# A four-layer trunk with ConvFFN: a shift read as a scalar from PSUM, and two adaLN sections moved from TensorE to VectorE

## The chip, the core and the metric

The kernel runs on one core of a Trainium2 chip. The metric is device time in microseconds from one execution of the whole program; lower is better. The core has five engines with queues of their own: TensorE (PE; matmul), VectorE (DVE), ScalarE (ACT), GpSimd (POOL) and SyncE (SP), which issues the loads. They meet through semaphores.

## The reference

One step of a trunk of four layers over 128 context tokens and 256 latent tokens with 1024 features. Each layer has a token mixer (gated MLP, pooling, attention, gated MLP) and a ConvFFN, and both are preceded by an RMSNorm with a shift and a scale and followed by a gate. These six vectors of a layer ("adaLN sections" of 1024 values, for two conditions) come from one large product. What matters here:

```python
def ada_params(cond, w, b):
    m = jax.nn.silu(cond) @ w + b
    return jnp.split(m[:, None, :], 6, axis=-1)

def conv_ffn(h, w_in, conv_w, conv_b, w_out):
    a, u = jnp.split(h @ w_in, 2, axis=-1)
    ap = jnp.pad(a, ((0, 0), (1, 1), (0, 0)))
    a = ap[:, :-2] * conv_w[0] + ap[:, 1:-1] * conv_w[1] + ap[:, 2:] * conv_w[2] + conv_b
    return (jax.nn.gelu(a) * u) @ w_out

def run_trunk(x, cond, is_context, cache_k, cache_v, weights):
    ...
        sh1, sc1, gt1, sh2, sc2, gt2 = ada_params(cond, w_ada[i], b_ada[i])
        h = rms_norm(x, g_mix[i]) * (1 + sc1) + sh1
        ...
        x = x + gt1 * y
        h = rms_norm(x, g_ffn[i]) * (1 + sc2) + sh2
        x = x + gt2 * conv_ffn(h, w_ffn_in[i], ffn_conv_w[i], ffn_conv_b[i], w_ffn_out[i])
```

Context tokens use one condition and latent tokens another; the inner width of the ConvFFN is 2816.

## The kernel before

Features lie on partitions, the 384 tokens along the free axis (`T` = 384). Every weight product runs in three passes of float32 parts (`mm3`, L631): high by high, low by high, high by low. The weights come as chunks of 128 x 1024, 582 in all, in the one order that `chunk_plan` (L90) writes down; SP loads them in that order (`load`, L313) into five buffers, so a chunk's place in the plan sets when it arrives. ScalarE rounds a weight chunk to its high part (`whi`, L338) and VectorE takes the remainder (`wlo`, L345), both in `w_split`, up to three chunks ahead of TensorE (`w_get`).

Among the weights stand the chunks of the adaLN sections. The table `ADA` (L39) says for each phase of a layer which sections, or which of a section's eight chunks, come along, and on which engine. "ad" goes to VectorE (`ada_dve`, L374): two instructions over 128 x 1024 with an accumulated sum (L380), a *pair* below. "ap" goes to TensorE (`ada_pe`, L389): four column-tiled products into one PSUM tile (L398), and after a section's last chunk a copy by ScalarE (L402), two transposes (L421) and an addition by VectorE. `weave` (L75) spreads the chunks evenly over the phase's weights, but for those at the edges (`EDGES`; in phase "fi" none after the last six weight chunks). After each `w_split` VectorE works off the pairs that have arrived (L348); `w_get` places the products of "ap" ahead of the next weight chunk's.

The phases used below are, for layer l: "fi" (first product of the ConvFFN, 22 feature tiles f of a and of u), "fo" (its second product), "nm" and "qkv" (norm, and the query/key/value product of the attention in layer 2; blocks b = 0, 2, 1 in this order, 2 holds the keys and values).

In `ffn` (L641) the norm's factor follows after the product: the operand holds x times its gain, next to two columns `T:TE` with the shift, so the PSUM tiles pa and pu hold the product and, in their last two columns, that of the shift for the two groups of tokens. The factor comes late: `stats` (sums of squares by TensorE, `ms` L524, the root), a diagonal R (L530) on VectorE, a product that spreads it over the partitions (`spread`, L536), and a copy to `rbs`. A pool of six PSUM banks holds pa and pu. Their epilogue, by feature: `epi_a` (a = pa x rbs, L657; the shifts' columns copied to `be`, L659 and L660; u = pu x rbs, L662), `epi_b` (on ScalarE a + shift into `ab` and the middle tap, on VectorE the two other taps `ct`, L676), `epi_c` (gelu on ScalarE, then gg = (u + shift of u) x gelu on VectorE, one instruction for each group, L685), and the split of gg into `gh` and `gl` (L567, L568). The epilogue of f runs while TensorE works on f + 1; that of f = 0 and 1 both while it works on f = 2, since the first four tiles (two features) are computed together.

Of the kernel before, what the change touches and what calls it, by code (L numbers as in the profile page):

```python
# [20 lines left out]
T = 384  # L21
# [15 lines left out]
# adaLN sections (layer, which of the six) computed along with the weights of a phase: by VectorE ("ad", features on  # L37
# partitions, dot products along the free axis) or by TensorE ("ap", column-tiled products)
# [18 lines left out]
# chunks of a phase that none of VectorE's sections follow, at its start and at its end  # L57
EDGES = {(0, "gv"): (2, 1), (0, "go"): (5, 0), (3, "gv"): (5, 2), "fi": (0, 6), (3, "go"): (5, 2)}

# the same for those of TensorE, at the end  # L60
# [4 lines left out]
# ---------------------------------------------------------------- packing  # L65


def out_chunks(fam, j, nk):
    """Two feature tiles at a time, but the last two one after the other."""
    n = (nk + 3) // 4  # L70
    return [(fam, j, m, kk) for m in range(3) for kk in range(n)] + [(fam, j, m, kk) for m in (3, 4)
                                                                    for kk in range((nk + 7) // 8)]


def weave(ws, es, lead, rest):  # L75
    """Spread es evenly over ws, but for the first `lead` and the last `rest`."""
    out, n, i = [], 0, 0
    total = sum(w[0] not in ("ad", "ap") for w in ws)
    for w in ws:
        out.append(w)  # L80
        if w[0] in ("ad", "ap"):
            continue
        i += 1
        m = min(len(es), max(0, len(es) * (i - lead) // max(1, total - lead - rest)))
        out += es[n:m]
        n = m
    return out


def chunk_plan():  # L90
    """Chunks of 128 x 1024 in the order in which the program loads them: (family, index)."""
# [126 lines left out]
def shape_consts():  # L218
    """Constants that depend on shapes alone: rope tables, window mask, a selection matrix."""
# [20 lines left out]
def pool_mix():  # L240
    """mix[t', g, t]: weight of token t' in the centred mean at t, less one where t' = t."""
# [17 lines left out]
def pool_sums():  # L259
    """Column sums of mix for each group of tokens (what a shift common to all its tokens is weighed with)."""  # L260
# [7 lines left out]
# ---------------------------------------------------------------- program  # L268


class Prog:
# [36 lines left out]
    # ---- stream of chunks  # L308
# [4 lines left out]
    def load(self, most=BUFS):  # L313
        """Start the loads for which there is room."""
# [14 lines left out]
    def w_split(self, upto, mid=None):  # L329
        """Round the coming chunks (ScalarE), run mid, take the remainders (VectorE)."""  # L330
# [38 lines left out]
    # ---- adaLN parameters  # L369
# [37 lines left out]
    def ada_spare(self, n):  # L407
        """At most n of VectorE's chunks, of those already loaded."""
# [19 lines left out]
    def ada_fill(self, n, fin=True):  # L428
        """At most n products of those already loaded; without fin, none that would have to close a section before."""
# [17 lines left out]
    # ---- norm  # L447
    def residual(self, d, ps, l, ty, after):
        """x_d += gate * ps, and what follows from x_d."""
# [9 lines left out]
    def square(self, d, acc):  # L459
        """Add the squares of x_d to acc; the last ones are only returned."""  # L460
# [18 lines left out]
    def rsqrt_steps(self, m, shape, y):  # L479
        """1/sqrt(m) by VectorE alone: an estimate from the exponent, refined to float32; one instruction at a time."""  # L480
# [22 lines left out]
    def rsqrt(self, m, shape):  # L503
        """1/sqrt(m), refined to float32."""
# [10 lines left out]
    def stats(self, *parts):  # L515
        """1/rms of each token (tokens on partitions) from tiles that add up to the squares."""
# [10 lines left out]
    def diag(self, r):  # L527
        """A diagonal of r for each token tile."""
# [10 lines left out]
    def gains(self, l, which):  # L539
        """g * (1 + sc) for both groups."""  # L540
# [8 lines left out]
    def put(self, ks, A, rb, hi, lo, l):  # L549
        """hi and lo of x * A * rb + B for some tiles."""  # L550
# [19 lines left out]
    def prep(self, l, which, extra=None):  # L570
        """What a norm's product needs of x_d, right after x_d is there: its squares, and x * g * (1 + sc) split in
        two, next to the shift's columns; the norm's factor follows after the product."""
# [24 lines left out]
    def norm(self, l, pr, bank):  # L597
        """Returns put(n), which makes h = rms_norm(x) * g * (1 + sc) + sh for the next n tiles."""
# [19 lines left out]
    def prep_squares(self, l):  # L618
        """The squares alone, for a norm before its product."""
# [10 lines left out]
    # ---- matrix products  # L630
    def mm3(self, outs, whl, rhl, first, last, nw=128):  # L631
        """Three passes for a set of (psum, weight column) with one k: hi*hi, lo*hi, hi*lo."""
# [7 lines left out]
    # ---- feed forward  # L640
    def ffn(self, l, pr, follow, stat_k):  # L641
        nc = self.nc
        hh, hl = self.hh[:, :, 0:TE], self.hl[:, :, 0:TE]
        with self.tc.tile_pool(name=f"ffn{l}", bufs=1) as fp:
# [3 lines left out]
            # a with a column of zeros on either side of each group  # L648
# [6 lines left out]
            def epi_a(f, pa, pu):  # L655
                a1 = self.tmp.tile([128, T], F32, tag="sq", name="a1")
                nc.vector.tensor_tensor(out=a1, in0=pa[:, 0:T], in1=rbs, op=ALU.mult)  # L657
                be = self.tmp.tile([128, 4], F32, tag="be", name="be")
                nc.vector.tensor_copy(be[:, 0:2], pa[:, T:TE])  # L659
                nc.vector.tensor_copy(be[:, 2:4], pu[:, T:TE])  # L660
                u1 = fp.tile([128, T], F32, tag="u1", name="u1", bufs=2)
                nc.vector.tensor_tensor(out=u1, in0=pu[:, 0:T], in1=rbs, op=ALU.mult)  # L662
                return f, a1, be, u1

            def epi_b(st):
                f, a1, be, _ = st
# [13 lines left out]
            def epi_c(st, t):  # L680
                _, _, be, u1 = st
                nc.scalar.activation(t, t, GELU)  # L682
                g = self.tmp.tile([128, T], F32, tag="gg", name="gg")
                for c, (t0, t1) in enumerate(GRPS):
                    nc.vector.scalar_tensor_tensor(out=g[:, t0:t1], in0=u1[:, t0:t1], scalar=be[:, 2 + c:3 + c],  # L685
# [38 lines left out]
    def out_proj(self, fam, gh, gl, nk, l, ty, after, banks=None, mid=None, after_chunk=-1):  # L724
        """Two feature tiles at a time, the last two one after the other; mid runs after one of the first chunks."""
# [16 lines left out]
    # ---- gMLP  # L742
    def gmlp(self, l, j, prep, pr=None, hook=None):
        """Layer 0 takes h from hh and hl. Later, hh and hl hold x * g * (1 + sc): the first columns of u come first, and
        the normed h for v goes to where the second half of the product's operand will be."""
# [153 lines left out]
    # ---- pooling  # L899
    def pool(self, l, j, prep, pr):  # L900
        """The product with the group's weights first (tokens on partitions), then the mean over the window less the
        token itself as a product with a matrix of constants. The norm's factor is a token's, so it goes in between; the
        shift is the same for all tokens of a group, so its product meets the constants' sums."""
# [72 lines left out]
    # ---- attention  # L976
    def attention(self, l, prep, norm):
# [3 lines left out]
        with self.tc.tile_pool(name=f"att{l}", bufs=1) as ap:  # L981
            # each head's queries (high parts over low parts); each key head's high and low parts, twice
# [56 lines left out]
            def heads(b, bank):  # L1039
                """Head norms, gains and rotation of a projected block, as steps to run one by one."""  # L1040
# [13 lines left out]
                def key_sums():  # L1054
                    # by way of where the keys' second copy will be
# [8 lines left out]
                def roots():  # L1064
                    # 1/rms; for the second half of the queries it meets their scores instead, with the scores' factor
# [10 lines left out]
                def turn(i):  # L1076
                    if b != 1:
                        scale(i)
                    if i == 0 and b < 2:
                        # the context's gain is in its keys  # L1080
# [66 lines left out]
            # A pair of heads at a time, in two parts: X has the scores of the middle token tile against all latent and  # L1147
            # cached keys, and of the context tile against the context; Y has those of the last token tile.
# [17 lines left out]
            def rs(s, y, i):  # L1166
                """The factor of the scores of both heads."""
# [5 lines left out]
            def maxima(s, y, between):  # L1173
                """The scores' maxima, with VectorE's other work in between."""
# [25 lines left out]
            def exps(s, y):  # L1200
                t = S.pop((s, y))
                nm, es, sm = St[s, y]
                if y and s % 2:
                    # the projected keys are no longer needed
# [377 lines left out]
```

## Time and profile before

| what | value |
|---|---|
| median of 3 runs | 1800.54 us (1800.51 to 1800.55) |
| span of the profiled execution | 1798.9 us (its own time is not listed; the span is 1.6 below the median) |
| TensorE / VectorE / ScalarE busy | 1778.0 / 1364.0 / 862.5 us |
| granted TensorE clock | 1.000 over the span |
| TensorE's longest wait | 9.0 us, for the first load |

Busy shares are averages over stages with different limits. Where an engine stood idle before an instruction, the timeline shows in brackets how long and which engine's result released it. A row "x2" in a timeline stands for two equal instructions that follow each other.

### The profile page before, as it was taken

Reading aid. Unit: us, or ns where it says so; the run is one execution under the profiler, and the core shown is the slowest. Engines: PE = TensorE matmul, PEld = TensorE weight load, DVE = VectorE, ACT = ScalarE, POOL = GpSimd, SP = SyncE. Lnnn points to the kernel's source line nnn. Section 1 sums busy time; section 2 is a strip of 40 time slices with the busy share of each in tenths; the row PEclk is TensorE's granted clock in tenths of the full one; section 3 lists DMA queues with packets and bytes.
Section 4 is the critical chain, followed back from the end, with each engine's and each line's share of the span. In section 5 each row is a group of like instructions: output and inputs, shape, how many; then the busy total and the mean of one; then the engine's idle time right before and its main releaser. Section 6 shows DMA issues by size and latency. Waiting matters only on the chain.

```text
span 1798.9 us, 27205 instructions
## 1 busy us (share of the span) xinstructions
PE 1778.0 (99%) x10458; PEld 1685.6 (94%) x10458; DVE 1364.0 (76%) x2568; ACT 862.5 (48%) x1470; POOL 1.8 (0%) x30
## 2 busy tenths in 40 slices
PE   7999999999999999999999999999999999999999
PEld 5799899999998999999678999999988999999999
DVE  5877688887776888776777788878776787888732
ACT  3634335554445555432568454544354443545431
POOL 0000000000000000000000000000000000000000
PEclk9999999999999999999999999999999999999999
DMA  8875565554553444365643444436546245444341
GB/s 321 281 243 178 211 219 182 184 177 157 205 182 118 152 153 164 135 211 184 241 171 124 145 154 154 162 135 211 193 161 213 96 163 188 141 145 148 123 148 58
DMA packets 87639, 311.67 MB, mean 173 GB/s; under 512 B 10451, under 2 KB 10963, under 8 KB 87253
## 3 DMA queue, kind: packets, MB, share of 16 engines
q1 hardware_dynamic: 87364, 309.92, 49.7%
q8 instruction: 82, 1.34, 0.3%
q14 instruction: 49, 0.39, 0.1%
q10 hardware_dynamic: 144, 0.01, 0.0%
HBM read 308.06 MB, written 1.84 MB: 172 GB/s over the span
## 4 chain that ended last, share of the span: by engine, by line
PE 96%; DVE 2%; ACT 1%; DMA 1%; issue 0%; DVEq 0%; ACTq 0%
PE mm L638 76%; PE mm L763 6%; PE S L1036 2%; PE S L638 1%; PE psa L398 1%; PE mm L807 1%; PE adaT L638 1%; PE mm L929 1%; PE psa L763 1%; PE adaT L763 1%; PE Tps L1036 1%; PE cs L521 1%; PE O L1256 0%; PE psa L638 0%; PE psa L1438 0%; PE Tps L1244 0%
## 5 line engine op out<-in xcount | busy, mean ns | idle before, releaser
L345 DVE TENSOR_TENSOR wlo<-wraw,whi 128x1024 fp32r<-128x1024 f32 (+2 forms) x390 | 466.0, 1201 | 212.2 <-ACT whi L338 207.1
L338 ACT ACTIVATE whi<-wraw 128x1024 fp32r<-128x1024 f32 (+2 forms) x390 | 400.7, 1036 | 388.4 <-PE mm L638 307.1
L638 PE MATMUL mm<-hh,whi 128*128 128x386 f32 (+1 forms) x1664 | 427.2, 342 | 0.0
L638 PE MATMUL mm<-hh,wlo 128*128 128x386 f32 (+1 forms) x1664 | 423.5, 339 | 0.0
L638 PE MATMUL mm<-hl,whi 128*128 128x386 f32 (+1 forms) x1664 | 421.2, 338 | 0.0
L638 PEld LDWEIGHTS mm<-hh,whi 128*128 128x128 f32 x1664 | 300.0, 188 | 7.9 <-issue 4.9
L638 PEld LDWEIGHTS mm<-hh,wlo 128*128 128x128 f32 x1664 | 303.4, 188 | 0.0
L638 PEld LDWEIGHTS mm<-hl,whi 128*128 128x128 f32 x1664 | 303.2, 188 | 0.0
L380 DVE SCALAR_TENSOR_TENSOR junk<-wraw,condb 128x1024 bf16<-128x1024 f32 x240 | 293.3, 1222 | 7.1 <-ACT condb L1500 2.7
L638 PE MATMUL mm<-gh,whi 128*128 128x384 f32 x704 | 193.6, 336 | 0.0
L638 PE MATMUL mm<-gh,wlo 128*128 128x384 f32 x704 | 193.6, 336 | 0.0
L638 PE MATMUL mm<-gl,whi 128*128 128x384 f32 x704 | 193.5, 336 | 0.0
L638 PEld LDWEIGHTS mm<-gh,wlo 128*128 128x128 f32 x704 | 128.5, 188 | 0.0
L638 PEld LDWEIGHTS mm<-gh,whi 128*128 128x128 f32 x704 | 128.5, 188 | 0.0
L638 PEld LDWEIGHTS mm<-gl,whi 128*128 128x128 f32 x704 | 128.4, 188 | 0.0
L682 ACT ACTIVATE ct<-ct 128x385 f32<-128x385 f32 x88 | 46.4, 528 | 156.7 <-DVE ct L676 156.6
L676 DVE SCALAR_TENSOR_TENSOR ct<-ab,par,ct 128x385 f32<-128x385 f32 x176 | 108.9, 621 | 12.2 <-ACT ct L674 8.2
L685 DVE SCALAR_TENSOR_TENSOR gg<-u,be,ct 128x128 f32<-128x128 f32 (+1 forms) x176 | 65.6, 416 | 47.6 <-ACT ct L682 47.6
L586 ACT ACTIVATE hh<-x,A 128x128 fp32r<-128x128 f32 x96 | 43.2, 457 | 102.5 <-DVE x L453 91.6
L672 ACT ACTIVATE ab<-a,be 128x128 f32<-128x128 f32 (+1 forms) x176 | 70.0, 446 | 28.9 <-DVE be L659 28.9
L657 DVE TENSOR_TENSOR a<-mm,rbs 128x384 f32<-128x384 f32 x88 | 48.7, 553 | 37.7 <-PE mm L638 31.8
L674 ACT ACTIVATE ct<-ab,par 128x385 f32<-128x385 f32 x88 | 62.7, 712 | 3.4
(302 smaller groups left out, 1987.6 us busy)
## 6 DMA issues: line engine op xcount, KB each, us to landing
wraw<-wts SPq DMA_DIRECT2D x562, 512.0 KB, 3.3
wraw<-wts SPq DMA_DIRECT2D x12, 256.0 KB, 2.5
wraw<-wts SPq DMA_DIRECT2D x8, 384.0 KB, 3.5
x<-x SPq DMA_DIRECT2D x4, 384.0 KB, 4.5
mx<-mix SPq DMA_DIRECT2D x1, 1280.0 KB, 8.1
y<-x SPq DMA_DIRECT2D x3, 384.0 KB, 3.1
condb<-condb SPq DMA_DIRECT2D x1, 1024.0 KB, 8.1
ws<-a_w_s SPq DMA_DIRECT2D x2, 512.0 KB, 4.2
```

The costliest lines, as they stand in the source:

```text
L338: nc.scalar.activation(hi[:, :n], t[:, :n], AF.Copy)
L345: nc.vector.tensor_tensor(out=lo[:, :n], in0=t[:, :n], in1=hi[:, :n].bitcast(F32), op=ALU.subtract)
L380: nc.vector.scalar_tensor_tensor(out=self.junk.bitcast(BF16), in0=w, scalar=1.0, in1=self.condb[:, c, :], op0=ALU.mult, op1=ALU.mult, accu ...
L638: nc.tensor.matmul(o, w[:, c:c + nw], r, start=(first and p == 0), stop=(last and p == 2))
L657: nc.vector.tensor_tensor(out=a1, in0=pa[:, 0:T], in1=rbs, op=ALU.mult)
L672: nc.scalar.activation(ab[:, p0:p1], a1[:, t0:t1], AF.Identity, bias=be[:, c:c + 1])
L674: nc.scalar.activation(t, ab[:, 1:T + 2], AF.Identity, scale=cw[1], bias=cb)
L676: nc.vector.scalar_tensor_tensor(out=t, in0=ab[:, i:i + T + 1], scalar=cw[i], in1=t, op0=ALU.mult, op1=ALU.add)
L682: nc.scalar.activation(t, t, GELU)
L685: nc.vector.scalar_tensor_tensor(out=g[:, t0:t1], in0=u1[:, t0:t1], scalar=be[:, 2 + c:3 + c], in1=t[:, t0 + c:t1 + c], op0=ALU.add, op1=A ...
L763: nc.tensor.matmul(ps[n][i], hs, w[p == 1][:, c:c + 512], start=(k == 0 and p == 0), stop=(k == 7 and p == 2))
L1036: nc.tensor.matmul(ps[i], hs, w[p == 1][:, c:c + 512], start=(k == 0 and p == 0), stop=(k == 7 and p == 2))
```

## The change

The columns of u's shift are no longer copied: gg takes its scalar straight from the PSUM tile pu. Those of a are copied by ScalarE instead of VectorE. And `ADA` is written anew: section (1, 2) moves from "ap" in layer 0's "fi" to "ad" there, section (2, 4) from "ap" in the attention's "qkv" to "ad" in layer 1's "fo", and the chunks of other "ad" sections shift between the phases of layers 0 and 1. Pairs by phase: layer 0 "fi" 19 (before 12, and 8 chunks on TensorE), "fo" 13 (12); layer 1 "fi" 13 (11), "fo" 19 (13). In "qkv" TensorE has 2 chunks (10). The rest of the file differs in comments alone; after line 659 numbers are one lower.

```diff
@@ ADA @@
-    (0, "fi"): [("ad", 1, 0), ("ad", 1, 4, 0, 4), ("ap", 1, 2)],
-    (0, "fo"): [("ad", 1, 4, 4, 8), ("ad", 1, 3)],
-    (1, "fi"): [("ad", 1, 5), ("ad", 2, 1, 0, 3)],
-    (1, "fo"): [("ad", 2, 1, 3, 8), ("ad", 2, 0)],
+    (0, "fi"): [("ad", 1, 2), ("ad", 1, 0), ("ad", 1, 4, 0, 3)],
+    (0, "fo"): [("ad", 1, 4, 3, 8), ("ad", 1, 3)],
+    (1, "fi"): [("ad", 1, 5), ("ad", 2, 1, 0, 5)],
+    (1, "fo"): [("ad", 2, 1, 5, 8), ("ad", 2, 0), ("ad", 2, 4)],
     (2, "nm"): [("ap", 2, 3, 0, 6)],
-    (2, "qkv"): [("ap", 2, 3, 6, 8), ("ap", 2, 4)],
+    (2, "qkv"): [("ap", 2, 3, 6, 8)],
@@ epi_a @@
-                be = self.tmp.tile([128, 4], F32, tag="be", name="be")
-                nc.vector.tensor_copy(be[:, 0:2], pa[:, T:TE])
-                nc.vector.tensor_copy(be[:, 2:4], pu[:, T:TE])
+                be = self.tmp.tile([128, 2], F32, tag="be", name="be")
+                nc.scalar.activation(be, pa[:, T:TE], AF.Copy)
...
-                return f, a1, be, u1
+                return f, a1, be, u1, pu[:, T:TE]
@@ epi_c @@
-                _, _, be, u1 = st
+                _, _, _, u1, bu = st
...
-                    nc.vector.scalar_tensor_tensor(out=g[:, t0:t1], in0=u1[:, t0:t1], scalar=be[:, 2 + c:3 + c],
+                    nc.vector.scalar_tensor_tensor(out=g[:, t0:t1], in0=u1[:, t0:t1], scalar=bu[:, c:c + 1],
```

How the order of instructions moves, at three places. VectorE in layer 0's ConvFFN from the last remainder ahead of f = 2, before (a, be, u: `epi_a` of f = 0 and 1; ct: the taps):

```order
L345 TENSOR_TENSOR wlo<-wraw,whi 128x1024
L380 SCALAR_TENSOR_TENSOR junk,prm<-wraw,condb 128x1024 x2
L657 TENSOR_TENSOR a_2505<-mm,rbs 128x384
L659 COPY be<-mm 128x2
L660 COPY be<-mm 128x2
L662 TENSOR_TENSOR u_2510<-mm,rbs 128x384
L657 TENSOR_TENSOR a_2512<-mm,rbs 128x384
L659 COPY be<-mm 128x2
L660 COPY be<-mm 128x2
L662 TENSOR_TENSOR u_2517<-mm,rbs 128x384
L345 TENSOR_TENSOR wlo<-wraw,whi 128x1024
L676 SCALAR_TENSOR_TENSOR ct<-ab_2344,par,ct 128x385 x2
```

And from the same remainder on after the change:

```order
L345 TENSOR_TENSOR wlo<-wraw,whi 128x1024
L657 TENSOR_TENSOR a_2515<-mm,rbs 128x384
L661 TENSOR_TENSOR u_2519<-mm,rbs 128x384
L657 TENSOR_TENSOR a_2521<-mm,rbs 128x384
L661 TENSOR_TENSOR u_2525<-mm,rbs 128x384
L345 TENSOR_TENSOR wlo<-wraw,whi 128x1024
L380 SCALAR_TENSOR_TENSOR junk,prm<-wraw,condb 128x1024 x2
L675 SCALAR_TENSOR_TENSOR ct<-ab_2348,par,ct 128x385 x2
L675 SCALAR_TENSOR_TENSOR ct<-ab_2349,par,ct 128x385 x2
L684 SCALAR_TENSOR_TENSOR gg<-u_2519,mm,ct 128x128
L684 SCALAR_TENSOR_TENSOR gg<-u_2519,mm,ct 128x256
L684 SCALAR_TENSOR_TENSOR gg<-u_2525,mm,ct 128x128
```

The four copies are gone, the pair has moved from ahead of the epilogues to between them, in front of the taps, and gg names the PSUM tile `mm`. Ahead of this place, before layer 0's ms, stand three pairs where one stood.

VectorE at the norm of layer 1's ConvFFN, before:

```order
L345 TENSOR_TENSOR wlo<-wraw,whi 128x1024
L380 SCALAR_TENSOR_TENSOR junk,prm<-wraw,condb 128x1024 x2
L345 TENSOR_TENSOR wlo<-wraw,whi 128x1024 x3
L380 SCALAR_TENSOR_TENSOR junk,prm<-wraw,condb 128x1024 x2
L524 TENSOR_SCALAR ms<-cs 128x3
L509 RECIPROCAL rs_5506<-rs_5505 128x3
```

And after:

```order
L345 TENSOR_TENSOR wlo<-wraw,whi 128x1024 x3
L380 SCALAR_TENSOR_TENSOR junk,prm<-wraw,condb 128x1024 x2
L345 TENSOR_TENSOR wlo<-wraw,whi 128x1024
L524 TENSOR_SCALAR ms<-cs 128x3
L509 RECIPROCAL rs_5462<-rs_5461 128x3
```

Before, two pairs stand among the phase's four remainders, the second right ahead of ms; after the change there is one, and the last remainder stands between it and ms.

TensorE in the first block of the query/key/value product, before (L1036: the product for three token tiles; L421 closes a section; L398: one adaLN chunk):

```order
L1036 MATMUL S<-whi,hl 128x512 x2
L1036 MATMUL Tps<-whi,hl 128x512
L421 MATMUL adaT<-ident,adarow 128x128 x2
L398 MATMUL psa<-wraw,cond 32x256 x4
L1036 MATMUL S<-whi,hh 128x512 x2
L1036 MATMUL Tps<-whi,hh 128x512
L1036 MATMUL S<-wlo,hh 128x512 x2
L1036 MATMUL Tps<-wlo,hh 128x512
L1036 MATMUL S<-whi,hl 128x512 x2
L1036 MATMUL Tps<-whi,hl 128x512
L1036 MATMUL S<-whi,hh 128x512 x2
```

And after, up to the first L398 that follows the norm's spread:

```order
L1035 MATMUL S<-whi,hl 128x512 x2
L1035 MATMUL Tps<-whi,hl 128x512
L1035 MATMUL S<-whi,hh 128x512 x2
L1035 MATMUL Tps<-whi,hh 128x512
L1035 MATMUL S<-wlo,hh 128x512 x2
L1035 MATMUL Tps<-wlo,hh 128x512
L1035 MATMUL S<-whi,hl 128x512 x2
L1035 MATMUL Tps<-whi,hl 128x512
L398 MATMUL psa<-wraw,cond 32x256 x4
```

Before, a chunk stands like this after every 12 rows of products, ten in the three blocks; after the change the first one comes behind 60 rows of products, one more follows, and the transposes stand no longer in the first block.

## Rows read from the trace of the kernel before

**Rows 1.** the page: busy time, share of the span and instructions of each engine

```profile
PE 1778.0 (99%) x10458; PEld 1685.6 (94%) x10458; DVE 1364.0 (76%) x2568; ACT 862.5 (48%) x1470; POOL 1.8 (0%) x30
```

**Rows 2.** timeline of TensorE, layer 0's ConvFFN: start, duration (us), engine, line, operation, tiles, size

```profile
272.04 0.81 PE L536 MATMUL adaT<-R,ones 128*128 128x384 f32 x2
...
273.80 0.52 PE L638 MATMUL mm<-hh,wlo 128*128 128x386 f32 x2
...
448.70 0.51 PE L638 MATMUL mm<-gh,whi 128*128 128x384 f32 x2
```

**Rows 3.** timeline of TensorE, layer 1's ConvFFN; in brackets the idle time before, and its releaser

```profile
589.33 0.88 PE L536 MATMUL adaT<-R,ones 128*128 128x384 f32 x2 [1.05 <-DVE R L530]
...
590.40 0.51 PE L638 MATMUL mm<-hh,wlo 128*128 128x386 f32 x2
...
759.91 0.51 PE L638 MATMUL mm<-gh,whi 128*128 128x384 f32 x2
```

**Rows 4.** timeline of VectorE, layer 1's second norm

```profile
583.84 1.23 DVE L345 TENSOR_TENSOR wlo<-wraw,whi 128x1024 fp32r<-128x1024 f32 x1 [3.01 <-ACT whi L338]
...
587.40 0.16 DVE L524 TENSOR_SCALAR ms<-cs 128x3 f32<-128x3 f32 x1
...
588.62 0.56 DVE L530 TENSOR_TENSOR R<-ident,rs 128x384 f32<-128x384 f32 x1
```

**Rows 5.** timeline of VectorE, layer 0's norm and the epilogues of f = 0 to 2

```profile
265.85 0.15 DVE L524 TENSOR_SCALAR ms<-cs 128x3 f32<-128x3 f32 x1
...
279.19 1.43 DVE L685 SCALAR_TENSOR_TENSOR gg<-u,be,ct 128x128 f32<-128x128 f32 x4
...
282.90 0.55 DVE L657 TENSOR_TENSOR a<-mm,rbs 128x384 f32<-128x384 f32 x1
283.37 0.15 DVE L659 COPY be<-mm 128x2 f32<-128x2 f32 x1
283.44 0.15 DVE L660 COPY be<-mm 128x2 f32<-128x2 f32 x1
...
285.10 1.21 DVE L380 SCALAR_TENSOR_TENSOR junk<-wraw,condb 128x1024 bf16<-128x1024 f32 x1
...
287.51 1.27 DVE L676 SCALAR_TENSOR_TENSOR ct<-ab,par,ct 128x385 f32<-128x385 f32 x2
...
291.93 0.55 DVE L657 TENSOR_TENSOR a<-mm,rbs 128x384 f32<-128x384 f32 x1
```

**Rows 6.** busy time by window, layer 1's second product: PE, PEld, DVE, ACT, POOL, clock, DMA

```profile
760.00:851.00 91.00, 91.00 (x527) 91.00 (x526) 65.23 (x104) 28.38 (x36) 0.00 (x0) 1.00 0.57 194
```

**Rows 7.** timeline of TensorE, the query/key/value product of layer 2

```profile
858.19 1.00 PE L1036 MATMUL S<-whi,hh 128*128 128x512 f32 x2 [0.88 <-ACT hh L558]
...
864.00 1.01 PE L1036 MATMUL S<-whi,hh 128*128 128x512 f32 x2 [0.54 <-ACT hh L558]
...
878.77 0.64 PE L398 MATMUL psa<-wraw,cond 128*32 128x256 f32 x8
...
915.04 0.49 PE L1108 MATMUL Tps<-ident,kd 128*128 128x128 f32 x3
```

**Rows 8.** timeline of ScalarE, the end of the same stretch

```profile
898.64 0.60 ACT L1292 ACTIVATE kv<-Tps 128x512 f32<-128x512 f32 x1 [0.15 <-PE Tps L1036]
...
912.62 1.03 ACT L1103 ACTIVATE kd<-kd 128x256 f32<-128x256 f32 x3 [1.35 <-DVE kd L1083]
...
915.57 0.37 ACT L1110 ACTIVATE kTc<-Tps,par 128x128 f32<-128x128 f32 x1 [1.40 <-PE Tps L1108]
```

**Rows 9.** groups of VectorE's instructions by line: busy us, mean ns | idle before, releasers

```profile
L657 DVE TENSOR_TENSOR a<-mm,rbs 128x384 f32<-128x384 f32 x88 | 48.7, 553 | 37.7 <-PE mm L638 31.8 <-ACT rbs L698 5.9
L568 DVE TENSOR_TENSOR gl<-gg,gh 128x384 fp32r<-128x384 f32 x88 | 48.2, 552 | 2.4 <-ACT gh L567 2.4
...
L685 DVE SCALAR_TENSOR_TENSOR gg<-u,be,ct 128x128 f32<-128x128 f32 x88 | 31.0, 352 | 47.6 <-ACT ct L682 47.6
...
L659 DVE COPY be<-mm 128x2 f32<-128x2 f32 x88 | 13.1, 149 | 0.0
```

More of the change, by code (lines that the diff above doesn't have):

```diff
@@ L657, in epi_a @@
                 nc.vector.tensor_tensor(out=a1, in0=pa[:, 0:T], in1=rbs, op=ALU.mult)
-                be = self.tmp.tile([128, 4], F32, tag="be", name="be")
-                nc.vector.tensor_copy(be[:, 0:2], pa[:, T:TE])
-                nc.vector.tensor_copy(be[:, 2:4], pu[:, T:TE])
+                be = self.tmp.tile([128, 2], F32, tag="be", name="be")
+                nc.scalar.activation(be, pa[:, T:TE], AF.Copy)
                 u1 = fp.tile([128, T], F32, tag="u1", name="u1", bufs=2)
                 nc.vector.tensor_tensor(out=u1, in0=pu[:, 0:T], in1=rbs, op=ALU.mult)
-                return f, a1, be, u1
+                return f, a1, be, u1, pu[:, T:TE]
             def epi_b(st):
-                f, a1, be, _ = st
+                f, a1, be, _, _ = st
                 cw = [self.par[:, PCOLS["cw"][0] + (3 * l + i) * NF + f:][:, 0:1] for i in range(3)]
```

## The prediction

> **What bounds the kernel now.** First the busy shares of the page: TensorE is at work for 1778.0 us of a span of 1798.9, VectorE for 1364.0, ScalarE for 862.5 [rows 1]. So an instruction taken from TensorE is worth its own length wherever the product behind it is ready, and VectorE can take work only where the stage leaves it room. Then TensorE's timeline at the three places that the change touches [rows 2, 3, 7] and VectorE's beside it [rows 4, 5]: a row with a bracket shows an engine that stood idle, and for whom; a row without one shows that TensorE had its operands in time. Last the groups of instructions by line, for what one instruction takes [rows 9].
>
> **Fewer chunks on TensorE in layer 0's first FFN product: -6.1 us.** Layer 0 has eight adaLN chunks and a pair of transposes (L421) there, layer 1 has none, and the work is otherwise the same. From the third product of f=2 to the first product of the second matrix layer 0 takes 273.80 to 448.70 = 174.90 [rows 2], layer 1 590.40 to 759.91 = 169.51 [rows 3]. The difference, 5.39, is seven chunks and the transposes. The eighth stands between the spread and that third product: 273.80 - 272.04 = 1.76 against 590.40 - 589.33 = 1.07, so 0.69. Sum 6.08. With 0.69 to 0.74 per chunk I use 0.72 below, and 0.35 for the transposes. The 169.51 hold 958 products, 48 to a step of f, so a step on TensorE is 8.49.
>
> **Layer 1's norm: -1.1.** Before, an adaLN pair stands ahead of ms (at 587.40, right behind the pair's 2.41), the diagonal R is done at 588.62 + 0.56 = 589.18, and the spread on TensorE has waited 1.05 [rows 3, 4]. In the new order three remainders (L345) come first, then the pair, then the last remainder and ms. Ahead of that remainder VectorE now idles 3.01 us for ScalarE [rows 4]; the pair's 2.41 fits in there. ms then starts when its sums are there, R ends by about 588.0, and the spread would be due at 589.33 - 1.05 = 588.28. The wait goes; next in line is TensorE's own product before it.
>
> **Eight of ten chunks out of the query/key/value product: -4.9 (4.0 to 6.2).** The stretch is 858.19 to 915.04 [rows 7]. In the part up to 878.77 three chunks and a pair of transposes lie; the first of them is followed by a wait of 0.54 for hh (864.00), so taking it away mostly lengthens that wait. That leaves 2 x 0.72 + 0.35 = 1.8, with a part of the first 2.0 (1.8 to 2.4). In the rest seven lie and five go, 5 x 0.72 = 3.6. But the transposes of the keys at 915.04 need a chain that starts with the copy of the keys (898.64, released by TensorE) and ends with ScalarE's copies at 912.62, which had waited 1.35 for VectorE [rows 8]. The three chunks ahead of 898.64 move this chain by 2.2; its middle is VectorE work among remainders, which loses some waits too. Bounds 2.2 and 3.6; I take the middle, 2.9.
>
> **What the moved sections cost.**
> (a) Before layer 0's ms two more pairs, 2 x 2.41 = 4.82 (a pair: 285.10 to 287.51 [rows 5]). R ended 1.78 after ms's start, as in layer 1 (587.40 to 589.18 [rows 4]), so at 267.63; now at 272.45. The spread is due at 272.04 [rows 2]. Wait +0.5; 0 if one of the pairs fits into idle time, 1.3 if a load is late.
> (b) u's shift stays in PSUM, so the bank of u is held until gg (L684). Six banks serve three features; f=3 on TensorE needs those of f=0. Before, gg of f=0 starts at 279.19, four of them 1.43 [rows 5]. Now the copies L659 and L660 are gone (two for each feature, 0.07 apart at 283.37 and 283.44: 0.26 for the four) but the new pair stands ahead of ct: 279.19 - 0.26 + 2.41 = 281.34, and two gg end at 282.06. Without the chunk TensorE's f=2 begins near 272.04 + 1.07 - 0.36 = 272.75, f=3's first product for u is due 8.49 + 0.18 later, at 281.42. Wait +0.7 (0 to 1.3). Later features have one epilogue each, half of this.
> (c) With a pair in every step a VectorE step takes 291.93 - 282.90 = 9.03 [rows 5], less 0.13 for the copies = 8.90 against TensorE's 8.49. VectorE begins f=3's step about 3.1 late, and falls back 0.41 in each of 14 further steps: 8.8. It may be some 8.8 late (the remainder of a chunk is done 8.5 us into the step and needed 17.35 after its start): +0.2, with ends 0 and 1.5. The later layers have no pair in every step: 13 over 16 steps in layer 1 make 8.90 - 3/16 x 2.41 = 8.45 on average, 11 in layer 2 make 8.15. Both are under 8.49, so no loss.
> (d) ScalarE's copy of a's shift (L659) must follow VectorE's a. The nearest rows give it 0 to the 0.37 of a 128x128 copy [rows 8]; with a pair in the step it is covered by the remainder and the pair on VectorE (3.5 us), without one VectorE waits for ct up to 0.4 longer in a step with over 1.5 to spare. Nothing.
> (e) The six further pairs during layer 1's second FFN product, 6 x 2.41 = 14.5, beside VectorE's 65.23 busy in 91.00 [rows 6]: 79.7 of 91, nothing. The loads are the same 582 chunks in another order, and SP still runs five ahead.
>
> **gg with its scalar in PSUM.** The trace has no such instruction. The bounds: 0, and the whole 0.149 of a copy of those columns [rows 9], twice per step; below nothing is excluded, as gg's tensors stay where they are. The nearest rows say 0: with a tensor from PSUM, L657 takes 553 ns, with all in SBUF, L568 takes 552 [rows 9]. I take 0. [...]
>
> **Sum**: 6.1 + 1.1 + 4.9 - 0.5 - 0.7 - 0.2 = 10.7. The profiled execution spans 1798.9; 1788.2 then. The median of the runs lies 1.6 above that span, so **1789.8**.
>
> **Rivals.**
> *The scalar from PSUM costs what a copy costs.* 0.30 per step: in layer 0 VectorE falls back 15 x (0.41 + 0.30) = 10.7, of which 8.8 - 3.1 = 5.7 is free, a loss of 5.0 where c has 0.2 to 0.5. That is 1794.3; at half the price 1792. For it: some price must be paid for the access; against: the equal rows above. Chance 0.14.
> *The chunks in the query/key/value product filled time TensorE would wait anyway.* The wait of 0.54 behind one of them is for it [rows 7]; that the row at 878.77 has no wait before it, and the products there none behind it, is against. That part then gives 2.5: 1792.2. Chance 0.08.
> *Layer 1's second FFN product leaves VectorE late for the next norm.* 79.7 of 91 busy leaves little at the end, where the last tiles go one by one; a pair or a pair and a half in front of the squares costs 3.5: 1793.3. Chance 0.05.
> *Slower: VectorE becomes the bound in all FFN layers.* The place is gg, which reads a PSUM bank while TensorE writes others. If gg went from 352 ns [rows 9] to double, a step is 0.70 longer: layer 0 loses 15 x 1.11 - 5.7 = 11, layer 1 18 x (0.70 - 0.04) - 5.7 = 6.2, layer 2 18 x (0.70 - 0.34) - 5.7 = 0.8, together 18 against 10.9 gained without c's 0.2: 1807.6. It decides from about 0.26 us per gg, where the losses come to 10.9. No row comes near. Chance 0.03.
> *More than forecast*: no new wait (1.4), and the whole 3.6 of the keys' stretch: 1787.7 and less. Chance 0.04. That the change does not move what it says is excluded by the two orders ahead.
>
> **How the numbers follow.** The forecast case has 0.66. Its own ends: the costs at their bounds (1787 to 1792). The first three rivals reach 1794.3, the last to 1787; the range 1786.8 to 1794.8 leaves out the slow case and the tails of the others, under 2 in 10. About 3.6 us, 0.2%, is what the measurement can tell. All but the slow case and part of the first rival lie more than that below 1800.5: faster 0.93, within 0.04, slower 0.03.
>
> **What would show it.** Right: no L398 in layer 0's first FFN product and 169 to 171 us for it; the spread in layer 1 without a wait; the stretch of queries, keys and values near 52 us, with the wait of ScalarE's kd copies on VectorE still there; waits of TensorE for banks (on gg) once in layer 0, under 1.5 us; gg at 350 ns. Wrong: gg above 420 ns, TensorE waiting for wlo in the later steps of layer 0, or a norm's spread waiting for R after layer 1.

## The result, and the profile after

The changed kernel takes **1789.79 us** (median of 4 runs, 1789.29 to 1790.51) against 1800.53 before: a ratio of 0.9937, 95% interval 0.9925 to 0.995. The forecast was 1789.8. The sum hit; its terms did not all hit, and their errors largely cancelled. The profiled execution spans 1787.8 us.

The page of the changed kernel, busy time of each engine (as [rows 1]):

```profile
PE 1766.3 (99%) x10326; PEld 1682.8 (94%) x10326; DVE 1387.9 (78%) x2456; ACT 873.9 (49%) x1556; POOL 1.8 (0%) x30
```

TensorE has 11.7 us less work, VectorE 23.9 more. TensorE's timeline of the changed kernel, from layer 0's spread to the transposes of the keys (as [rows 2, 3, 7]):

```profile
271.43 0.88 PE L536 MATMUL adaT<-R,ones 128*128 128x384 f32 x2 [0.22 <-DVE R L530]
...
272.50 0.52 PE L638 MATMUL mm<-hh,wlo 128*128 128x386 f32 x2
...
280.64 0.52 PE L638 MATMUL mm<-hh,whi 128*128 128x386 f32 x2
...
391.79 0.62 PE L638 MATMUL mm<-hh,wlo 128*128 128x386 f32 x2 [0.23 <-DVE wlo L345]
...
400.69 0.62 PE L638 MATMUL mm<-hh,wlo 128*128 128x386 f32 x2
...
409.60 0.62 PE L638 MATMUL mm<-hh,wlo 128*128 128x386 f32 x2
...
418.50 0.62 PE L638 MATMUL mm<-hh,wlo 128*128 128x386 f32 x2
...
443.74 0.51 PE L638 MATMUL mm<-gh,whi 128*128 128x384 f32 x2
...
583.16 0.81 PE L536 MATMUL adaT<-R,ones 128*128 128x384 f32 x2
...
850.06 0.64 PE L398 MATMUL psa<-wraw,cond 128*32 128x256 f32 x8 [0.84 <-DMA wraw<-wts]
...
852.42 1.00 PE L1035 MATMUL S<-whi,hh 128*128 128x512 f32 x2 [0.87 <-ACT hh L558]
...
857.65 1.00 PE L1035 MATMUL S<-whi,hh 128*128 128x512 f32 x2 [0.50 <-ACT hh L558]
...
903.64 0.73 PE L1107 MATMUL Tps<-ident,kd 128*128 128x128 f32 x3
```

Layer 0 no longer has a chunk behind the spread (1.07 to the third product instead of 1.76). From 391.79 on TensorE stalls four times, 8.90 or 8.91 apart. The last three stalls are too short to have a bracket; they show in the starts (the first product of the row at 400.69 starts 0.48 behind the product before it, elsewhere it is 0.18). Layer 1's spread (583.16) has no bracket any more.

VectorE's timeline in layer 0 (as [rows 5]):

```profile
281.16 1.44 DVE L684 SCALAR_TENSOR_TENSOR gg<-u,mm,ct 128x128 f32<-128x128 f32 x4
...
284.87 0.55 DVE L657 TENSOR_TENSOR a<-mm,rbs 128x384 f32<-128x384 f32 x1
...
293.78 0.55 DVE L657 TENSOR_TENSOR a<-mm,rbs 128x384 f32<-128x384 f32 x1
...
383.01 0.55 DVE L657 TENSOR_TENSOR a<-mm,rbs 128x384 f32<-128x384 f32 x1
...
390.51 1.22 DVE L345 TENSOR_TENSOR wlo<-wraw,whi 128x1024 fp32r<-128x1024 f32 x1 [0.19 <-ACT whi L338]
...
392.12 0.55 DVE L657 TENSOR_TENSOR a<-mm,rbs 128x384 f32<-128x384 f32 x1
```

A step with a pair is 293.78 - 284.87 = 8.91, and the remainder that TensorE wants at 391.41 (0.35 behind the start of its f = 16, 391.06) is done at 391.73. The groups of instructions by line (as [rows 9]) have gg at 356 ns:

```profile
L657 DVE TENSOR_TENSOR a<-mm,rbs 128x384 f32<-128x384 f32 x88 | 48.6, 552 | 20.5 <-PE mm L638 14.5 <-ACT rbs L697 5.7
...
L684 DVE SCALAR_TENSOR_TENSOR gg<-u,mm,ct 128x128 f32<-128x128 f32 x88 | 31.3, 356 | 49.1 <-ACT ct L681 49.1
```

The span by stretches, from the starts of the spreads and of the second products' first instructions on TensorE's timeline (us). "Layer 0, 2nd" reaches to layer 1's spread, so it has that norm's wait in it; "layer 1, 2nd" reaches to the attention's spread, "attention" to the spread behind it.

| run | to layer 0's spread | layer 0, 1st | layer 0, 2nd | layer 1, 1st | layer 1, 2nd | attention |
|---|---|---|---|---|---|---|
| before | 272.04 | 176.66 | 140.63 | 170.58 | 96.52 | 182.01 |
| the change | 271.43 | 172.31 | 139.42 | 170.51 | 96.96 | 176.69 |
| difference | -0.61 | -4.35 | -1.21 | -0.07 | +0.44 | -5.32 |
| forecast | +0.5 | -5.2 | -1.1 | 0 | 0 | -4.9 |

Behind that, up to the end, both take the same (760.5).

### The profile page after: what moved, and what is told of

Read it like the earlier page. It is cut to its first block, busy times and chain, and to the rows that moved or that the text cites. A ratio compares the mean times of both kernels' runs of the same rounds, so it can differ in the third digit from the quotient of the medians.

```text
span 1787.8 us, 26990 instructions
## 1 busy us (share of the span) xinstructions
PE 1766.3 (99%) x10326; PEld 1682.8 (94%) x10326; DVE 1387.9 (78%) x2456; ACT 873.9 (49%) x1556; POOL 1.8 (0%) x30
## 4 chain that ended last, share of the span: by engine, by line
PE 84%; DVE 10%; ACT 3%; issue 2%; DMA 1%; SPq 0%; DVEq 0%; ACTq 0%
PE mm L638 65%; PE mm L762 6%; DVE junk L380 3%; DVE wlo L345 2%; ACT whi L338 1%; PE S L638 1%; PE mm L806 1%; DMA wraw<-wts 1%; DVE ct L675 1%; PE S L1035 1%; PE psa L398 1%; PE adaT L638 1%; PE mm L928 1%; PE psa L762 1%; PE adaT L762 1%
## 5 line engine op out<-in xcount | busy, mean ns | idle before, releaser
L380 DVE SCALAR_TENSOR_TENSOR junk<-wraw,condb 128x1024 bf16<-128x1024 f32 x272 | 332.2, 1221 | 7.6 <-ACT condb L1499 2.7
L684 DVE SCALAR_TENSOR_TENSOR gg<-u,mm,ct 128x128 f32<-128x128 f32 (+1 forms) x176 | 66.3, 419 | 49.1 <-ACT ct L681 49.1
```

The costliest lines, as they stand in the source:

```text
L380: nc.vector.scalar_tensor_tensor(out=self.junk.bitcast(BF16), in0=w, scalar=1.0, in1=self.condb[:, c, :], op0=ALU.mult, op1=ALU.mult, accu ...
```

## The experiments

Runs of one job are on one chip; each is compared with runs of before beside it, whose medians were 1801.29 (the first four), 1800.56 (the next four) and 1801.36 (the last three). Single runs of one kernel lie up to 5 us apart there (before, beside the second four: 1798.5 to 1803.43), so stretches of the trace are read beside the medians.

**The table alone.** Of the changed kernel only the new `ADA`; the epilogue as before.

```diff
-                be = self.tmp.tile([128, 2], F32, tag="be", name="be")
-                nc.scalar.activation(be, pa[:, T:TE], AF.Copy)
+                be = self.tmp.tile([128, 4], F32, tag="be", name="be")
+                nc.vector.tensor_copy(be[:, 0:2], pa[:, T:TE])
+                nc.vector.tensor_copy(be[:, 2:4], pu[:, T:TE])
```

> The new table of sections with the old epilogue (both shifts copied by VectorE). Theory: in layer 0's first ConvFFN product VectorE sets the pace at the end; its step with a pair is 9.03 us here instead of 8.90, so it falls back 15 x 0.13 = 2.0 us more, and TensorE loses that: 1791.8 us (1791.2 to 1792.4), with TensorE waiting for wlo in about 8 steps instead of 4. Rival: what TensorE loses in layer 0 comes from the PSUM bank that gg now holds; then it is free of it here: 1788.1 us or less, no stall for wlo.

Measured 1791.36 us (ratio 0.9945, 0.9933 to 0.9958). Layer 0's first product takes 174.07, 1.76 more than with the change, and the waits for wlo are six, the first at f = 14. TensorE's timeline of this run:

```profile
374.06 0.62 PE L638 MATMUL mm<-hh,wlo 128*128 128x386 f32 x2 [0.28 <-DVE wlo L345]
383.10 0.62 PE L638 MATMUL mm<-hh,wlo 128*128 128x386 f32 x2 [0.31 <-DVE wlo L345]
...
419.44 0.62 PE L638 MATMUL mm<-hh,wlo 128*128 128x386 f32 x2 [0.28 <-DVE wlo L345]
```

The stalls are 9.03 to 9.24 apart here: they follow VectorE's step. No bank is held until gg in this kernel, so the rival falls.

**The epilogue alone.** The changed epilogue with the table of before.

> The old table with the new epilogue (a's shift copied by ScalarE, u's read from PSUM). Theory: VectorE has room in every step, so the copies it saves and the scalar from PSUM are worth nothing: 1800.5 us within 0.5, gg within 10 ns of before. Rival 1: the held bank makes TensorE wait once per layer at f = 3, 0.7 us each: 1802 to 1803. Rival 2: a shorter step on VectorE is worth something by itself (earlier loads): under 1799.5.

Measured 1800.87 us (0.9999, 0.999 to 1.0008). Layer 0's first product takes 176.66 as before, layer 1's 170.56, and gg 356 ns. The new epilogue is worth nothing where VectorE has room, and the held bank costs nothing. (The attention of the profiled execution is 2.8 longer; that is told in the last section.)

**The attention's section alone.** The change with layer 0's two rows of `ADA` as before.

```diff
-    (0, "fi"): [("ad", 1, 2), ("ad", 1, 0), ("ad", 1, 4, 0, 3)],
-    (0, "fo"): [("ad", 1, 4, 3, 8), ("ad", 1, 3)],
+    (0, "fi"): [("ad", 1, 0), ("ad", 1, 4, 0, 4), ("ap", 1, 2)],
+    (0, "fo"): [("ad", 1, 4, 4, 8), ("ad", 1, 3)],
```

> The change without its rows for layer 0: layer 0 as before (one section on TensorE), layer 1 and the attention as changed. Theory: the norm of layer 1 gives 1.2 and the query/key/value product 4.9 net of a 0.4 us wait for a load in front of it: 1794.4 us (1793.6 to 1795.2). Rival: the chunks of the query/key/value product filled time in which TensorE would wait: 1797 us.

Measured 1794.02 us (0.9962, 0.9949 to 0.9974). The stretches: 176.66, 139.42, 170.51, 96.52, 176.85. So layer 1's norm gives its 1.21 and the attention 5.16, and neither hangs on layer 0's rows. The 0.44 in layer 1's second product is not here with the same 19 pairs. It comes and goes between runs whose loads have the order of the change (96.52 in two of them, 96.96 to 97.30 in three); in the profile of the change TensorE waits 0.84 for a load there (850.06).

**Layer 0's section alone.** The change with the rows of layer 1 and of "qkv" as before.

> The change with its rows for layer 0 alone; layer 1 and the attention as before. Theory: eight chunks and the transposes give 6.1, the norm's wait and VectorE's pace take 2.1: 1796.5 us (1795.8 to 1797.2), with the four stalls at the end of the product as in the whole change. Rival: these stalls come from loads that the other rows of the table move; then 1794.8 us, without them.

Measured 1796.4 us (0.9972, 0.9963 to 0.9981). The first product takes 172.27, the next stretch 140.63 (so the norm's 1.05 of waiting is back), the attention 182.30. The first wait for wlo is at f = 16 as in the change. The rival falls: the stalls need no row of another layer.

**u's shift copied to SBUF by ScalarE.**

```diff
+                bu = self.tmp.tile([128, 2], F32, tag="bu", name="bu")
...
-                return f, a1, be, u1, pu[:, T:TE]
+                nc.scalar.activation(bu, pu[:, T:TE], AF.Copy)
+                return f, a1, be, u1, bu
```

> The changed kernel, but u's shift is copied to SBUF by ScalarE too, so gg reads no PSUM and holds no bank. Theory: neither the bank nor the scalar's place cost anything; TensorE still waits for wlo in about four steps from f = 16 on: 1789.8 us (1789.2 to 1790.6), gg within 10 ns of 352 for the 128-wide one. Rival: the held bank is what makes TensorE late in layer 0; then no wait for wlo there, the first product takes 169.5 to 170.5 from its third product on, and 1788 us.

Measured 1791.42 us (0.9951, 0.9937 to 0.9964). The first product takes 172.21, within 0.1 of the change, with the same waits for wlo: neither the held bank nor the scalar's place matters (gg 352 ns). Its median is 1.6 above that of the change, which was not expected (the intervals overlap; the profiled run, 1792.99, is the slowest of four). In the profile 2.3 stand in the next stretch, 141.73, and 0.7 of them are a wait: ScalarE's new copy waits for VectorE's u, the taps start later, VectorE leaves the last steps about 1.3 us later than in the change, and some 13 us into the second product TensorE waits for wlo. ScalarE's timeline and then TensorE's:

```profile
441.95 0.17 ACT L663 ACTIVATE bu<-mm 128x2 f32<-128x2 f32 x1 [0.29 <-DVE u L662]
```

```profile
457.93 0.62 PE L638 MATMUL mm<-gh,wlo 128*128 128x384 f32 x2 [0.53 <-DVE wlo L345]
```

The rest is no wait. Behind that place TensorE is busy without a break here and with the change, at a granted clock of 1.00 in both, but has 229 products in 40 us where the change has 233 (windows of this run, then of the change; columns as in [rows 6]). Why they are slower stays open.

```profile
470.00:510.00 40.00, 40.00 (x229) 40.00 (x228) 35.34 (x60) 18.54 (x31) 0.00 (x0) 1.00 0.66 212
```

```profile
470.00:510.00 40.00, 40.00 (x233) 40.00 (x232) 34.25 (x57) 18.55 (x31) 0.00 (x0) 1.00 0.63 213
```

**Sixteen pairs in each of layer 0's products.**

```diff
-    (0, "fi"): [("ad", 1, 2), ("ad", 1, 0), ("ad", 1, 4, 0, 3)],
-    (0, "fo"): [("ad", 1, 4, 3, 8), ("ad", 1, 3)],
+    (0, "fi"): [("ad", 1, 2), ("ad", 1, 0)],
+    (0, "fo"): [("ad", 1, 4), ("ad", 1, 3)],
```

> The changed kernel with three pairs moved from layer 0's first ConvFFN product (16 pairs now) to its second (16). Theory: VectorE's pace is the cause of the loss in layer 0; with a step without a pair here and there it never falls 8.6 us behind, no wait for wlo is left, and the 1.7 us come back: 1788.0 us (1787.4 to 1788.8), the stretch from the third product of f = 2 on 169.5 instead of 171.2. Rival: the loss comes from something else in the stage, or the second product with 16 pairs takes it back: 1789.8.

Measured 1788.99 us (0.9936, 0.9923 to 0.9948). The first product falls to 170.51, and no wait for wlo is left in it: VectorE's pace was the cause. But the second stretch grows from 139.42 to 141.20, with waits for wlo at its start and near its end:

```profile
455.24 0.61 PE L638 MATMUL mm<-gh,wlo 128*128 128x384 f32 x2 [0.64 <-DVE wlo L345]
...
523.41 0.44 PE L638 MATMUL mm<-gh,wlo 128*128 128x384 f32 x1 [0.46 <-DVE wlo L345]
```

1.80 gained, 1.78 given back: the rival that named the second product was right. Ahead of the first of these waits VectorE does a pair (444.53 to 446.94) before the epilogue of the last feature, where the change has none.

**Seventeen and fifteen, none at the second product's edges.**

```diff
+    (0, "fi"): [("ad", 1, 2), ("ad", 1, 0), ("ad", 1, 4, 0, 1)],
+    (0, "fo"): [("ad", 1, 4, 1, 8), ("ad", 1, 3)],
...
+EDGES = {(0, "gv"): (2, 1), (0, "go"): (5, 0), (0, "fo"): (2, 3), (3, "gv"): (5, 2), "fi": (0, 6), (3, "go"): (5, 2)}
```

> The changed kernel with two pairs moved from layer 0's first ConvFFN product to its second (17 and 15), and there none in the first two and the last three chunks, where the run with sixteen pairs waited for wlo. Theory: the first product then loses 0.5 at most instead of 1.7, and the second nothing, since VectorE starts it late but without a pair in its way: 1788.5 us (1787.8 to 1789.3), about 1.3 under the changed kernel in the same job. Rival: VectorE's work of the two products together is what counts, and what one gives back the other takes: the same as the changed kernel within 0.5.

Measured 1791.13 us (0.9942, 0.9928 to 0.9956), above the changed kernel in the same job. The first product again takes 170.51, the second stretch 142.65. The place of the loss can be seen on three engines. VectorE does two pairs and only then the residual (x) of a finished tile:

```profile
513.82 1.22 DVE L380 SCALAR_TENSOR_TENSOR junk<-wraw,condb 128x1024 bf16<-128x1024 f32 x1
...
517.11 1.23 DVE L380 SCALAR_TENSOR_TENSOR junk<-wraw,condb 128x1024 bf16<-128x1024 f32 x1
...
518.47 0.74 DVE L453 SCALAR_TENSOR_TENSOR x<-mm,prm,x 128x128 f32<-128x128 f32 x2
```

With the change VectorE does one pair there, and the residual starts 514.66 - 443.74 = 70.92 behind the second product's start, against 518.47 - 442.09 = 76.38 here (with sixteen pairs 516.41 - 441.50 = 74.91). VectorE's row of the change:

```profile
514.66 0.73 DVE L453 SCALAR_TENSOR_TENSOR x<-mm,prm,x 128x128 f32<-128x128 f32 x2
```

ScalarE, whose next weights stand behind that tile's work, idles 5.26 (3.70 with the change) and rounds them late:

```profile
518.85 0.90 ACT L586 ACTIVATE hh<-x,A 128x128 fp32r<-128x128 f32 x2 [5.26 <-DVE x L453]
...
523.10 2.72 ACT L338 ACTIVATE whi<-wraw 128x1024 fp32r<-128x1024 f32 x3
```

And TensorE waits:

```profile
524.20 0.44 PE L638 MATMUL mm<-gh,whi 128*128 128x384 f32 x1 [1.20 <-ACT whi L338]
525.46 0.44 PE L638 MATMUL mm<-gh,wlo 128*128 128x384 f32 x1 [0.82 <-DVE wlo L345]
```

**The attention's last gate section on VectorE.** As with sixteen pairs, and section (2, 5) in layer 2's ConvFFN.

```diff
-    (2, "at"): [("ap", 2, 2), ("ap", 2, 5)],
-    (2, "fi"): [("ad", 3, 1), ("ad", 3, 2, 0, 3)],
-    (2, "fo"): [("ad", 3, 0), ("ad", 3, 2, 3, 8)],
+    (2, "at"): [("ap", 2, 2)],
+    (2, "fi"): [("ad", 2, 5), ("ad", 3, 1)],
+    (2, "fo"): [("ad", 3, 0), ("ad", 3, 2)],
```

> As the one with sixteen pairs, and section (2, 5) moves from TensorE in the attention to VectorE in layer 2's first ConvFFN product (16 pairs there, 16 in the second). Theory: a chunk on TensorE is worth 0.74 where TensorE does not wait; the attention has few waits, so eight chunks and the transposes give 4 to 6: 1783.0 us (1782 to 1784.5). Rival: the attention's chunks fill time in which TensorE waits for the softmax: 1787 us.

Measured 1788.7 us (0.994, 0.9924 to 0.9955), no better than with sixteen pairs. The attention falls by 1.14 only (175.53 from 176.67), not by 4 to 6, and layer 2's second product takes 102.29 where the change has 101.30. TensorE's waits in the attention, added up from the brackets, grow from 5.9 with sixteen pairs to 9.0. So among the steps of the softmax most of a chunk's time is time in which TensorE would wait anyway; in the query/key/value product it stands in the way (5.32 for eight chunks and the transposes).

**No adaLN section but (2, 3) in the attention.** Section (2, 2) goes too; 20 pairs in layer 0's second product, 16 and 20 in layer 1's. The line of `chunk_plan` that sets two chunks of the attention's output product ahead of that section's last six goes too.

> As the one before, and section (2, 2) too goes to VectorE: 20 pairs in layer 0's second product, 16 and 20 in layer 1's. Nothing of the attention's adaLN chunks is left but section (2, 3). Theory: another 3 to 6 from TensorE, less some VectorE pace in layer 1 (16 pairs instead of 13): 1779 us (1777 to 1782). Rival: without chunks to fill in, the attention waits for its softmax, and gains nothing over the one before: 1783 to 1785.

Measured 1805.46 us (1.0027, 1.0015 to 1.0039), slower than before. The attention gives next to nothing more (175.32; 1.3 of it are slower products behind its spread, 3.76 from 867.36 to 871.12 for what takes 2.45 in the run before), and layer 0's second stretch grows to 152.49 and layer 1's to 101.78. TensorE's timeline has the same wait as above, larger:

```profile
480.29 0.62 PE L636 MATMUL mm<-gh,whi 128*128 128x384 f32 x2 [2.97 <-ACT whi L336]
...
531.21 0.44 PE L636 MATMUL mm<-gh,whi 128*128 128x384 f32 x1 [3.29 <-ACT whi L336]
```

Behind each of these two waits some 1.5 us more are lost to slower products; the last section has their starts, and the granted clock behind the first wait.

**The copy of a's shift on VectorE, u's read from PSUM.**

```diff
-                nc.scalar.activation(be, pa[:, T:TE], AF.Copy)
+                nc.vector.tensor_copy(be, pa[:, T:TE])
```

> The changed kernel, but the copy of a's shift goes back to VectorE; u's is still read from PSUM. Theory: a step with a pair takes 8.97 us instead of 8.90, the first wait for wlo comes one or two steps earlier, and layer 0 loses 0.5 to 1.0 more; in the steps without a pair ScalarE's chain starts sooner and nothing is lost: 1790.6 us (1790.0 to 1791.4). Rival: ScalarE's copy costs more on the chain to ct than it saves on VectorE; then 1789.3 or less, and fewer waits for wlo.

Measured 1790.53 us (0.9943, 0.993 to 0.9955), with 172.94 in layer 0's first product, 0.7 more than the changed kernel beside it (172.21), as the theory had it. TensorE's first two stalls on wlo:

```profile
382.38 0.62 PE L638 MATMUL mm<-hh,wlo 128*128 128x386 f32 x2
...
391.55 0.62 PE L638 MATMUL mm<-hh,wlo 128*128 128x386 f32 x2 [0.41 <-DVE wlo L345]
```

The first is too short for a bracket (382.38 is 0.42 behind the product before it, elsewhere 0.18); it is at f = 15, one step earlier than in the change, and from the second on they stand 8.96 or 8.97 apart. But ScalarE's copy has a price as well, as the rival said: without it the epilogues of f = 0 and 1 end earlier. gg of f = 0 starts 280.17 - 270.74 = 9.43 behind the spread, with the change 281.16 - 271.43 = 9.73.

**The changed kernel again.**

> The changed kernel itself, to have its time on the same chip as the two others: 1789.8 us within 1, and the same four stalls at the end of layer 0's first product.

Measured 1788.92 us (0.9933, 0.9921 to 0.9946), 172.21, 139.43 and 176.58 in the three stretches, and the same four stalls. None of the versions is clearly faster than it. Unlike in the first profile of this kernel, layer 0's spread does not wait for R here:

```profile
271.62 0.81 PE L536 MATMUL adaT<-R,ones 128*128 128x384 f32 x2
```

## Why the prediction was right, point by point

**Eight chunks out of layer 0: -6.1, confirmed.** 0.69 behind the spread, as worked out; and in the runs that have no stall the first product takes 170.51, which is 6.15 under before.

**Layer 1's norm: -1.1; measured -1.21**, and it comes with the rows of layer 1 alone.

**The query/key/value product: -4.9; measured -5.3 at the end.** The total was nearly right, two steps were not. The first removed chunk was to lengthen the wait for hh; from the first product to that wait's end it took 864.00 - 858.19 = 5.81 before and 857.65 - 852.42 = 5.23 now, with a wait of 0.50 instead of 0.54 [rows 7]. So 0.58 of its 0.7 came back. And the chain of the keys was to hold TensorE up. From the spread to the transposes 58.61 became 53.01, 5.60 of at most 6.1. ScalarE's copies do wait for VectorE, longer than before [rows 8]:

```profile
902.96 1.03 ACT L1102 ACTIVATE kd<-kd 128x256 f32<-128x256 f32 x3 [3.09 <-DVE kd L1082]
```

But TensorE starts the first transpose at 903.64 without a wait; the last starts when ScalarE's last copy is done (902.96 + 1.03 = 903.99), and the three take 0.73 instead of 0.49 [rows 7]. So this chain cost 0.2 to 0.3, not the 0.7 by which 2.9 lies under 3.6. I had read ScalarE's wait of 1.35 as one of TensorE's; no row of before had TensorE waiting there.

**The new waits: 1.4 forecast, 2.1 measured, by another split.** (a) The norm of layer 0: 0.22 of waiting; the stretch from the second a0T product (20.75 before, 19.75 after) to the spread is 0.39 longer, for 0.5. That is not steady: in the second profile of the same kernel the stretch takes 271.62 - 20.37 = 251.25, as before (251.29), the lower bound that (a) gave. (b) **The step that failed: the bank of u that gg holds.** It was to cost 0.7 at f = 3, by the assumption that f = 3 takes the banks of f = 0. TensorE's first two products of f = 3, one for a and one for u, start from 280.64 on without a wait, and gg of f = 0 only at 281.16. So f = 3 cannot have u's bank of f = 0. The built programs say which it has: before the change those of a and u of f = 0, as I assumed; after it the two banks of a, of f = 0 and of f = 1, while the two of u go to f = 4, a step later. The engines that an instruction waits for fit that: the first products of f = 3 wait for ScalarE alone (its copies of a's shift), those of f = 4 (below the line of dots) for VectorE too.

```
L638 MATMUL mm<-hh,whi 128x386 [waits Activation_49] x2
...
L638 MATMUL mm<-hh,whi 128x386 [waits DVE_49,Activation_49]
L638 MATMUL mm<-hh,whi 128x386 [waits DVE_49,PE_49]
```

(c) VectorE's pace was to cost 0.2; it cost 1.73 (171.24 from the third product on, against 169.51 [rows 3]). This is the term that was mis-sized most. The step was right to 0.01 us (8.90 worked out), and so nearly was what VectorE may be late (8.6, for 8.8): in the step that starts at 383.01 it is 8.94 behind TensorE (whose f = 14 starts at 374.07), and the remainder comes 0.32 late. What was wrong is where it starts. VectorE begins f = 3's step at 284.87, 4.23 behind TensorE's 280.64, not 3.1. 0.7 of the difference is the bank's wait, which would have held TensorE back. The other 0.43 is ScalarE's copy of a's shift, which (d) had counted as covered: gg of f = 0 starts 9.73 behind the spread instead of the 9.30 worked out, and with the copy back on VectorE 9.43, which is 9.30 and that engine's two copies.

**The scalar in PSUM: nothing, confirmed to 4 ns.** gg takes 356 ns against 352, and the larger group 483 against 479.

**Why the sum came out.** The changed stretches give 0.39 - 4.35 - 1.21 - 0.07 + 0.44 - 5.32 = -10.1, for -10.7 forecast. The rest of the profile's 11.1 is 1.0 us before 20.75 us, ahead of anything that changed; it moves from run to run (the same product starts between 19.05 and 20.77 in the runs above). In the second profile the stretches give -10.6. Part of the hit is luck of that size, and part is that the bank's 0.7 and the keys' chain, which were too high, stood against VectorE's pace, which was too low.

**The signs.** One that was named for a wrong forecast came: TensorE does wait for wlo in the later steps of layer 0. Of those named for a right one the wait on gg did not come, and layer 0's first product takes 172.31, not 169 to 171. The time stayed close because the cost was only 1.73.

**The rivals.** VectorE can become the bound of the ConvFFN and make the kernel slower than before, though not by gg: the run with 20 pairs in the second products was (1805.46), part of it by the slower products behind the waits, some 1.5 us each. That layer 1's second product with 19 pairs would delay the next norm did not come true (96.96, and 96.52 in other runs with the same pairs). Chunks that fill waiting time are real as well, but among the softmax's steps, not in the stretch that this change touched.

## What to carry to other kernels

Before work moves to an engine with room, take its step in that stage, the bound engine's step, and how late the first may be; the loss is what the lag exceeds, so the lag at the start counts as much as the slope. A stage's average share says too little: in layer 0's second product 13 pairs cost nothing and 16 cost 1.8, and layer 1's took 19 for nothing. Where a pair stands matters: ahead of the last epilogue it delays the next remainder (TensorE waited 0.64 for it with sixteen pairs), and in front of a tile's residual it holds up ScalarE and the next weights (5.26 of idle time with seventeen and fifteen, 3.70 with the change). And a product taken from the bound engine is worth its length only where no wait stands behind it: about 0.7 us per chunk in one stage, 0.14 in another (1.14 / 8).

## What the runs showed of the hardware that was not expected

In two profiled runs slower products followed a longer wait. In the profiled run of the epilogue alone a load was late before the query/key/value product's second chunk, and TensorE waited 1.76 for hh instead of 0.54. The products behind that wait took about 0.63 us each instead of 0.39 until 868, at a mean granted clock of 0.60 over that stretch. TensorE's timeline, and the windows ahead of, in and behind it (columns as in [rows 6]):

```profile
864.23 1.28 PE L1035 MATMUL S<-whi,hh 128*128 128x512 f32 x2 [1.76 <-ACT hh L558]
865.31 0.63 PE L1035 MATMUL Tps<-whi,hh 128*128 128x512 f32 x1
...
868.73 0.39 PE L1035 MATMUL Tps<-whi,hh 128*128 128x512 f32 x1
```

```profile
855.44:864.00 8.56, 6.16 (x31) 3.72 (x28) 5.67 (x12) 3.93 (x7) 0.00 (x0) 1.00 0.85 320
864.00:868.00 4.00, 3.76 (x9) 2.78 (x10) 3.75 (x10) 2.45 (x6) 0.00 (x0) 0.60 0.72 249
868.00:916.00 48.00, 47.75 (x256) 34.05 (x255) 33.60 (x79) 22.23 (x38) 0.00 (x0) 1.00 0.61 204
```

That attention takes 184.81 in all, 2.8 more than before: 1.2 of it is the longer wait, the rest goes with the slower products.

The run with no section but (2, 3) shows it again. Behind the wait of 2.97 the products of the second matrix start 0.32 us apart instead of 0.17 until 484.87, at a mean granted clock of 0.65. Behind the wait of 3.29 they start 0.32 apart as well, from 532.99 to 536.19. The windows ahead of, in and behind the first of these stretches:

```profile
470.00:480.29 10.29, 7.32 (x44) 7.00 (x42) 8.32 (x18) 5.02 (x12) 0.00 (x0) 1.00 0.56 186
480.29:484.80 4.51, 3.87 (x12) 3.55 (x13) 4.48 (x6) 1.41 (x2) 0.00 (x0) 0.65 0.36 116
484.80:494.00 9.20, 9.20 (x54) 9.20 (x54) 8.78 (x13) 2.13 (x2) 0.00 (x0) 0.99 0.89 281
```
